# Gated linear recurrence in a hybrid layer: convolution by halves, the whole gate projection ahead of the block's products

## The chip, the cores and the metric

One core of a Trainium2 chip. The metric is the device time of one execution in microseconds (us), as the median of several runs.

## The reference, cut to what matters

One layer is computed for two sequences of 1024 tokens with the same weights. The normalised input is projected, four mixers work on columns of the projection, and their outputs are merged. Two mixers matter here. The gated linear recurrence (RG-LRU) has 512 channels in 4 blocks of 128:

```python
xc = centred_dwconv(u, conv_w) + conv_b            # 4 taps
xb = xc.reshape(bsz, L, LRU_BLOCKS, LRU_BLOCK_W)
for d, rev in enumerate((False, True)):
    r = sigmoid(einsum('blhi,hij->blhj', xb, w_a[d]) + b_a[d])
    i = sigmoid(einsum('blhi,hij->blhj', xb, w_x[d]) + b_x[d])
    log_a = -LRU_C * softplus(-lam[d]) * r
    drive = sqrt(-expm1(2.0 * log_a)) * (i * xc)
    _, h = associative_scan(_linear_combine, (exp(log_a), drive), axis=1, reverse=rev)
    hs.append(h)
return (hs[0] + hs[1]) * silu(gate)
```

The other is the gated delta rule. For each head and chunk of 64 tokens it needs the inverse of a unit triangular matrix (`triangular_solve(a_mat + eye, eye)`).

## The kernel before, in words

The whole kernel is one core's program. Channels lie on the 128 partitions and the 1024 tokens of a sequence along a row. An fp32 product is made of three: each operand is split into a high and a low part, and hi·hi, hi·lo and lo·hi are summed in a PSUM bank of 128x512. A projection of 128 channels is 2 halves of tokens with 24 matmuls each (`proj_steps`); each half ends in one bank with tag `pj`.

The change lies in a stage that each sequence goes through once. It has 3 `pj`, 2 `lr` and 3 `dn` banks. `weave` records three or four generators in turn, each by its declared length:

- `lru`: the four blocks of the recurrence, one after the other (`lru_block`, 8 calls in all);
- `cor`: the inverses of the delta rule for two pairs of heads (`dn_core1`, L540 to L676);
- early projections of gates for later stages (`pre_gates`; tiles `fg`, evicted by ACT and multiplied by DVE);
- in the first sequence, `s5_rot`, whose tiles are called `E`.

The order that is recorded is not yet the order on the engines. A scheduler reorders the instructions of the whole stage by its own estimate of their times, and then every engine (and SP, which issues most DMAs) works through its list strictly in order. So a matmul that is not ready holds up all matmuls behind it. Almost every instruction is recorded through one helper, so its line in the profile is L54; the names of tiles tell what it is.

A block of the recurrence projects its input into `up` (`conv_in`), convolves it on DVE into `xc` (one tensor_scalar and three scalar_tensor_tensor on 128x1024, `conv`), casts `xc` to its high part `xh` on ACT and subtracts on POOL for the low part `xl`. Then it records half of its gate projection (24 matmuls, evicted into `sg` by ACT and DVE), the first products of `r`, the other half of the gate, and the rest: for each direction `r` and `i`, two halves of 3 matmuls, each half in an `lr` bank that ACT empties with a sigmoid. ACT, POOL and DVE then form a, r and i, ending in a scan on DVE.

A pair in `dn_core1` is a chain. DVE forms the matrices from rows (`rl`, `sl`), PE multiplies the keys (`dn<-sl`), small diagonal blocks of 32x32 go to DRAM (`lan_d`, L582) and come back as `Nf` (L588). Then 31 steps of substitution run on DVE, two instructions each: `tm<-sl,sl` (a product) and `sl<-sl,tm` (a subtraction), with rows that grow from 31 to 256 elements and shrink again. The result goes to `lan_d` (L601) and comes back in pieces (L635), and only then can the matmuls `dn<-sl,LE` run, 8 for each direction of each head (the profile shows the 8 as x16). The text calls the first such group of a pair LE0 and the next one LE1.

Of the kernel before, what the change touches and what calls it, by code (L numbers as in the profile page):

```python
# [7 lines left out]
F32 = mybir.dt.float32  # L8
F32R = mybir.dt.float32r
I32 = mybir.dt.int32  # L10
AF = mybir.ActivationFunctionType
ALU = mybir.AluOpType
# [5 lines left out]
T = 1024  # L18
# [15 lines left out]
def tile_hybrid_trunk(ctx: ExitStack, tc: tile.TileContext, A):  # L34
# [55 lines left out]
    def after(i, j):  # L90

        tc.add_manual_dep(i.ins, j.ins.name,
                          mybir.DependencyInfo(mybir.DependencyClass.NoSync, mybir.DependencyReason.DATA),
                          reason="program order")

    def mm(*a, **kw):
        PE.matmul(*a, **kw)

    def transpose(*a):
        PE.transpose(*a)  # L100
# [1 line left out]
    def act(out, in_, func, **kw):  # L102
        return S.activation(out=out, in_=in_, func=func, **kw)

    def tt(eng, out, a, b, op):
        eng.tensor_tensor(out, a, b, op)

    def ts(eng, out, a, s1, s2, o1, o2=None):
        if o2 is None:
            eng.tensor_scalar(out, a, s1, None, o1)  # L110
        else:
            eng.tensor_scalar(out, a, s1, s2, o1, o2)

    def stt(out, a, s, b, o1, o2):
        V.scalar_tensor_tensor(out, a, s, b, o1, o2)
# [5 lines left out]
    HALVES = (slice(0, 512), slice(512, 1024))  # L121
# [107 lines left out]
    def run(gen):  # L229
        for _ in gen:  # L230
            pass
# [103 lines left out]
        proj_cm(xn, wp, w_in, c0, 128, evac)  # L335

    def conv(out, up, cw, bias=None, first=None):
        if first is S:
            act(out, up[:, 0:T], AF.Copy, scale=cw[:, 0:1])
        elif bias is None:  # L340
            ts(V, out, up[:, 0:T], cw[:, 0:1], None, ALU.mult)
        else:
            ts(V, out, up[:, 0:T], cw[:, 0:1], bias, ALU.mult, ALU.add)
        for j in range(1, 4):
            stt(out, up[:, j:j + T], cw[:, j:j + 1], out, ALU.mult, ALU.add)


    def misc(s, xn, wp, pl):
# [457 lines left out]
    def lru_block(s, b, xn, wp, pl):  # L806
        two = ("r", "i", "sg")
        wt = lambda shape, tag, dt=F32: pl.tile(shape, dt, tag=tag, name=nm(tag), bufs=2 if tag in two else 1)
        up = wt([128, T + 4], "up")
        conv_in(xn, wp, up, LRU_X + b * 128)  # L810
        yield
        xc = wt([128, T], "xc")
        conv(xc, up, lru_cw[:, b], lru_cb[:, b:b + 1])
        xh, xl = wt([128, T], "xh", F32R), wt([128, T], "xl", F32R)
        S.copy(xh, xc)
        tt(G, xl, xc, xh.bitcast(F32), ALU.subtract)

        def srcs(raw):
            v = raw[:, :512].rearrange("p (a d c) -> p a d c", a=2, d=2)
            yield v[:, 0], A["lru_w_a"][0, :, b].rearrange("d i j -> i d j")  # L820
            yield v[:, 1], A["lru_w_x"][0, :, b].rearrange("d i j -> i d j")
        hi, lo = split_tile(pl, 512, srcs, 512, "lw", 1, 1)
        sg = wt([128, T], "sg")
        gate = gate_steps(xn, wp, LRU_G + b * 128, sg)

        def half():
            for _ in range(8):
                next(gate, None)
        half()
        yield 0.4  # L830
        hv = []
        for d in range(2):
            gts = []
            for gi, bias in ((0, lru_ba), (1, lru_bx)):
                r = wt([128, T], ("r", "i")[gi])
                mi = slice((gi * 2 + d) * 128, (gi * 2 + d + 1) * 128)
                for hf in range(2):
                    sl = slice(hf * 512, (hf + 1) * 512)
                    p = bank("lr")
                    for n, (a, x) in enumerate(((hi, xh), (hi, xl), (lo, xh))):  # L840
                        mm(p, a[:, mi], x[:, sl], start=(n == 0), stop=(n == 2))
                    act(r[:, sl], p, AF.Sigmoid, bias=bias[:, d, b:b + 1])
                gts.append(r)
                if gi == 0:
                    if d == 0:
                        half()
                        run(gate)
                    yield 0.4
            r, ig = gts
            j = d * 4 + b  # L850
            tt(G, ig, ig, xc, ALU.mult)
            a = wt([128, T], "a")
            act(a, r, AF.Exp, scale=sp8n[:, j:j + 1])
            act(r, r, AF.Tanh, scale=sp8[:, j:j + 1])
            a2 = wt([128, T + 4], "up")[:, 0:T]
            act(a2, a, AF.Square)
            stt(r, a2, 1.0, r, ALU.add, ALU.mult)
            act(r, r, AF.Sqrt)
            tt(V, ig, ig, r, ALU.mult)
            if d == 0:  # L860
                V.tensor_tensor_scan(ig, a, ig, 0.0, ALU.mult, ALU.add)
            else:
                V.tensor_tensor_scan(ig[:, ::-1], a[:, ::-1], ig[:, ::-1], 0.0, ALU.mult, ALU.add)
            hv.append(ig)
            yield
        tt(G, hv[0], hv[0], hv[1], ALU.add)
        tt(V, sg, hv[0], sg, ALU.mult)
        put_y(sg, s, 0, b)
        yield 0.01
# [879 lines left out]
```

## Time and profile before

| | us |
|---|---|
| median of 3 runs (lowest to highest) | 3104.76 (3102.79 to 3108.0) |
| the profiled execution | 3103.76 |
| its span, first to last instruction | 3101.5 |
| PE busy in it | 2875.3 |
| mean granted TensorE clock | 0.966 |

The span stands 2.26 us below the time of the same execution. In the profile a line names the engine, the operation and the tiles it writes and reads (`out<-in`), and in brackets how long the engine stood idle before it and what released it. A clock of 1.00 is 2.4 GHz, 0.50 is 1.2 GHz. The stage of the first sequence lies at about 300 to 700 us of the span, that of the second at about 1780 to 2150 us.

### The profile page before, as it was taken

What the parts mean: (1) busy time and instruction counts of PE and PEld (TensorE: products, weight loads), DVE (VectorE), ACT (ScalarE), POOL (GpSimd) and SP (SyncE); (2) the same over time, 40 slices, a digit from 0 to 9 for tenths busy, and PEclk for the clock granted to TensorE, in tenths of its full rate; (3) what the DMA queues carried; (4) which work ended last, traced back from release to release, by engine and by line L of the source; (5) the groups of instructions that cost most, each with busy time, mean ns of one, the idle gap of its engine ahead of it and who ended that gap; (6) DMA issues with size and microseconds to landing.
All of it is one profiled execution on the core that took longest, in us unless ns stands there. A gap on an engine that the chain in (4) does not pass through costs nothing. (4 is left out here: it accounts for less than half of the span.)

```text
span 3101.5 us, 42101 instructions
## 1 busy us (share of the span) xinstructions
PE 2875.3 (93%) x15386; PEld 2373.6 (77%) x15386; DVE 1877.1 (61%) x3569; ACT 1286.2 (41%) x1969; POOL 1043.0 (34%) x796
## 2 busy tenths in 40 slices
PE   6999979898989999999999998989897999999998
PEld 5787767677778787878778876767776887788877
DVE  7576887738662464665654467773867245566545
ACT  5644546534432432332444465553443233333223
POOL 2343565434332231121443333343433212211123
PEclk9999989999999999999999998999998999999999
DMA  5344535353332754553553342524333263565343
GB/s 111 102 153 142 153 104 182 92 162 121 121 112 74 214 162 157 176 194 124 182 160 109 102 137 73 165 80 160 117 120 104 74 192 104 183 216 192 105 156 124
DMA packets 449391, 427.37 MB, mean 138 GB/s; under 512 B 126848, under 2 KB 340384, under 8 KB 449184
## 3 DMA queue, kind: packets, MB, share of 16 engines
q1 hardware_dynamic: 403200, 374.07, 39.2%
q10 hardware_dynamic: 45984, 50.61, 4.7%
q8 instruction: 121, 1.98, 0.3%
q14 instruction: 86, 0.70, 0.1%
HBM read 306.87 MB, written 117.70 MB: 137 GB/s over the span
## 5 line engine op out<-in xcount | busy, mean ns | idle before, releaser
L54 PE MATMUL pj<-xn,hi 128*128 128x512 f32 x4608 | 1471.2, 399 | 20.2 <-ACT y L54 5.7
L54 POOL TENSOR_TENSOR lo<-raw,hi 128x512 fp32r<-128x512 f32 x432 | 600.9, 1394 | 1451.8 <-ACT hi L54 1298.3
L54 PEld LDWEIGHTS pj<-xn,hi 128*128 128x128 f32 x4608 | 869.7, 191 | 206.1 <-ACT y L54 6.1
L54 PE MATMUL pj<-xn,lo 128*128 128x512 f32 x2304 | 912.5, 396 | 1.3 <-POOL lo L54 1.3
L54 ACT CAST hi<-raw 128x512 fp32r<-128x512 f32 x432 | 265.2, 618 | 650.8 <-PE pj L54 482.2
L54 PEld LDWEIGHTS pj<-xn,lo 128*128 128x128 f32 x2304 | 439.5, 191 | 99.5 <-issue 5.0
L54 ACT ACT_TABLE_LOAD x201 | 257.9, 1283 | 118.2 <-DVE Ab L54 54.6
L54 PE MATMUL pj<-yh,hi 128*128 128x512 f32 x576 | 239.8, 417 | 4.5 <-ACT yh L54 4.4
L54 PE MATMUL pj<-yl,hi 128*128 128x512 f32 x576 | 225.8, 393 | 1.0 <-DVE yl L54 1.0
L54 PE MATMUL pj<-yh,lo 128*128 128x512 f32 x576 | 226.0, 393 | 0.0
L54 DVE TENSOR_TENSOR_SCAN w<-E,v 64x512 f32<-64x512 f32 x64 | 97.9, 1529 | 85.2 <-PE s L54 84.3
L54 DVE TENSOR_TENSOR sg<-sg,pj 128x512 f32<-128x512 f32 x128 | 87.6, 684 | 93.4 <-PE pj L54 65.6
L54 PE MATMUL pj<-hi,mh 128*128 128x512 f32 x384 | 124.3, 400 | 6.7 <-ACT mh L54 4.1
L54 PEld LDWEIGHTS pj<-yh,hi 128*128 128x128 f32 x576 | 109.6, 190 | 23.9 <-ACT yh L54 5.2
L54 PEld LDWEIGHTS pj<-yh,lo 128*128 128x128 f32 x576 | 108.7, 189 | 23.8
L54 PEld LDWEIGHTS pj<-yl,hi 128*128 128x128 f32 x576 | 109.5, 190 | 19.9 <-DVE yl L54 2.6
L54 ACT ACTIVATE fg<-pj,bmg 128x512 f32<-128x512 f32 x112 | 76.3, 687 | 116.4 <-PE pj L54 104.2
L54 ACT ACTIVATE vn<-r,beta 128x128 f32<-128x128 f32 x128 | 40.7, 365 | 169.5 <-DVE vs L54 167.3
L54 POOL TENSOR_TENSOR dcv<-dcv,dsg 128x1024 f32<-128x1024 f32 x24 | 60.4, 2518 | 144.3 <-ACT dsg L54 103.5
L54 PE MATMUL pj<-hi,xn 128*128 128x256 f32 x512 | 97.9, 290 | 10.0 <-DVE vt L54 10.0
L54 DVE TENSOR_TENSOR yl<-yr,yh 128x512 fp32r<-128x512 f32 x80 | 59.9, 753 | 76.3 <-ACT yh L54 76.1
L54 DVE SCALAR_TENSOR_TENSOR dcv<-dup,dn_cw,dcv 128x1024 f32<-128x1024 f32 x72 | 96.0, 1333 | 5.5 <-ACT dcv L54 2.5
(373 smaller groups left out, 4469.1 us busy)
## 6 DMA issues: line engine op xcount, KB each, us to landing
raw<-in_w_in_dram SPq DMA_DIRECT2D x176, 256.0 KB, 2.9
sl<-rows_d SPq DMA_DIRECT2D x128, 256.0 KB, 6.5
raw<-in_w_merge_gate_dram SPq DMA_DIRECT2D x128, 256.0 KB, 2.9
gs_d<-fg ACTq DMA_DIRECT2D x112, 256.0 KB, 2.1
sg<-gs_d SPq DMA_DIRECT2D x112, 256.0 KB, 2.7
sl<-qkv_d SPq DMA_DIRECT2D x40, 512.0 KB, 5.5
raw<-in_w_branch_dram SPq DMA_DIRECT2D x64, 256.0 KB, 3.4
yr<-ysp SPq DMA_DIRECT2D x64, 256.0 KB, 3.1
```

Source lines behind the costliest of these rows:

```text
L54: i = f(*a, **kw)
```

## The change

The convolution works on halves of 512 tokens, and the cast and the subtraction follow each half. The whole gate projection is recorded ahead of the products. The first product of a block gets an order dependency (no semaphore) on the last matmul of the gate. What is computed stays the same.

```diff
@@ mm
+    lastmm = [None]
+
     def mm(*a, **kw):
-        PE.matmul(*a, **kw)
+        lastmm[0] = PE.matmul(*a, **kw)
+        return lastmm[0]
@@ conv
     def conv(out, up, cw, bias=None, first=None):
+        n = out.shape[1]
         if first is S:
-            act(out, up[:, 0:T], AF.Copy, scale=cw[:, 0:1])
+            act(out, up[:, 0:n], AF.Copy, scale=cw[:, 0:1])
...
         for j in range(1, 4):
-            stt(out, up[:, j:j + T], cw[:, j:j + 1], out, ALU.mult, ALU.add)
+            stt(out, up[:, j:j + n], cw[:, j:j + 1], out, ALU.mult, ALU.add)
@@ lru_block
-        conv(xc, up, lru_cw[:, b], lru_cb[:, b:b + 1])
         xh, xl = wt([128, T], "xh", F32R), wt([128, T], "xl", F32R)
-        S.copy(xh, xc)
-        tt(G, xl, xc, xh.bitcast(F32), ALU.subtract)
+        for sl in HALVES:
+            conv(xc[:, sl], up[:, sl.start:sl.stop + 3], lru_cw[:, b], lru_cb[:, b:b + 1])
+            S.copy(xh[:, sl], xc[:, sl])
+            tt(G, xl[:, sl], xc[:, sl], xh[:, sl].bitcast(F32), ALU.subtract)
...
         half()
+        half()
+        run(gate)
+        dense = lastmm[0]
         yield 0.4
...
-                        mm(p, a[:, mi], x[:, sl], start=(n == 0), stop=(n == 2))
+                        i = mm(p, a[:, mi], x[:, sl], start=(n == 0), stop=(n == 2))
+                        if dense:
+                            after(i, dense)
+                            dense = None
...
                 if gi == 0:
-                    if d == 0:
-                        half()
-                        run(gate)
                     yield 0.4
```

Since the scheduler orders the whole stage anew, more moves than the diff shows. Three places follow.

On PE, at the first products of block 1 of the first sequence (`pj_3700` and `pj_3756` are the two halves of that block's gate, `lr_` the banks of `r`), before:

```order
L54 MATMUL pj_3700<-xn_7_101,hi_3695 128x512 x2
L54 MATMUL pj_3700<-xn_7_101,lo_3696 128x512
L54 MATMUL lr_3744<-xh_3676,hi_3681 128x512
L54 MATMUL lr_3749<-xh_3676,hi_3681 128x512
L54 MATMUL pj_3756<-xn_0_94,hi_3689 128x512 x2
L54 MATMUL lr_3744<-xl_3677,hi_3681 128x512
L54 MATMUL lr_3744<-xh_3676,lo_3682 128x512
L54 MATMUL lr_3749<-xl_3677,hi_3681 128x512
L54 MATMUL lr_3749<-xh_3676,lo_3682 128x512
L54 MATMUL pj_3756<-xn_0_94,lo_3690 128x512
```

and in the changed kernel, where `pj_3739` is the second half of the gate:

```order
L54 MATMUL pj_3739<-xn_7_101,hi_3707 128x512 x2
L54 MATMUL pj_3739<-xn_7_101,lo_3708 128x512
L54 MATMUL lr_3785<-xh_3678,hi_3693 128x512
L54 MATMUL lr_3785<-xl_3679,hi_3693 128x512
L54 MATMUL lr_3785<-xh_3678,lo_3694 128x512
L54 MATMUL lr_3790<-xh_3678,hi_3693 128x512
L54 MATMUL lr_3790<-xl_3679,hi_3693 128x512
L54 MATMUL lr_3790<-xh_3678,lo_3694 128x512
L54 MATMUL pj_3856<-xn_0_94,hi_3845 128x512 x2
```

The products moved from behind the first half of the gate to behind both, 24 matmuls later.

On PE, around LE0 of the first pair of the first sequence (`dn_3900`), before:

```order
L54 MATMUL lr_4014<-xh_3676,lo_3682 128x512
L54 MATMUL pj_4059<-xn_0_94,hi_4048 128x512 x2
L54 MATMUL pj_4059<-xn_0_94,lo_4049 128x512
...
L54 MATMUL pj_4059<-xn_3_97,hi_4048 128x512 x2
L54 MATMUL pj_4059<-xn_3_97,lo_4049 128x512
L54 MATMUL dn_3900<-sl_3789,LE_3787 64x64 x8
L54 MATMUL pj_4059<-xn_4_98,hi_4054 128x512 x2
```

and in the changed kernel, where it is `dn_3912`:

```order
L54 MATMUL pj_3885<-xn_7_101,lo_3852 128x512
L54 MATMUL lr_4021<-xh_3678,hi_3693 128x512
L54 MATMUL lr_4021<-xl_3679,hi_3693 128x512
L54 MATMUL dn_3912<-sl_3801,LE_3799 64x64 x8
L54 MATMUL lr_4021<-xh_3678,lo_3694 128x512
L54 MATMUL lr_4026<-xh_3678,hi_3693 128x512
```

LE0 moved 16 matmuls forward in PE's list: 12 of a projection and 4 products now stand behind it. In the first pair of the second sequence it moved 8 forward, and in the second pairs it kept its place (LE0 of the first sequence is PE's row 1543 in both lists).

On DVE, at the end of the substitution of the same pair (`tm` and `sl`; `r_3743` is the `r` of block 1, `sg` and `fg` products of gates), before:

```order
L54 TENSOR_TENSOR tm_3731<-sl_3314,sl_3315 128x135
L54 SCALAR_TENSOR_TENSOR r_3743<-up_3822,r_3743 128x1024
L54 TENSOR_TENSOR sl_3315<-sl_3315,tm_3731 128x27x5
L54 TENSOR_TENSOR sg_3687<-sg_3687,pj_3756 128x512
...
L54 TENSOR_TENSOR tm_3783<-sl_3314,sl_3315 128x31
L54 TENSOR_TENSOR sl_3315<-sl_3315,tm_3783 128x31
L54 TENSOR_TENSOR i_3807<-i_3807,r_3743 128x1024
```

and in the changed kernel:

```order
L54 TENSOR_TENSOR sl_3321<-sl_3321,tm_3772 128x27x5
L54 TENSOR_TENSOR sg_3699<-sg_3699,pj_3739 128x512
...
L54 TENSOR_TENSOR tm_3795<-sl_3320,sl_3321 128x31
L54 TENSOR_TENSOR sl_3321<-sl_3321,tm_3795 128x31
L54 SCALAR_TENSOR_TENSOR r_3784<-up_3834,r_3784 128x1024
L54 TENSOR_TENSOR fg_3881<-fg_3881,pj_3856 128x512
```

The work on `r` moved behind the last step of the substitution. At the other end of this chain another `r` (of block 0) moved out too, ahead of the first step.

## Rows read from the trace of the kernel before

**Rows 1.** The page, part 1: busy time of each engine.

```profile
PE 2875.3 (93%) x15386; PEld 2373.6 (77%) x15386; DVE 1877.1 (61%) x3569; ACT 1286.2 (41%) x1969; POOL 1043.0 (34%) x796
```

**Rows 2.** PE's waits at 300 to 700 us: total us, times, longest.

```profile
PE lr L54 <- ACT xh L54: 16.2, 3, 7.5
PE lr L54 <- ACT r L54: 5.4, 1, 5.4
...
PE lr L54 <- POOL xl L54: 2.3, 2, 1.8
```

**Rows 3.** PE's waits at 1780 to 2160 us, same columns.

```profile
PE lr L54 <- ACT xh L54: 7.3, 1, 7.3
...
PE lr L54 <- POOL xl L54: 4.0, 2, 2.2
```

**Rows 4.** ACT's timeline: start us, us, engine, line, operation, idle before.

```profile
400.16 1.04 ACT L54 CAST xh<-xc 128x1024 fp32r<-128x1024 f32 x1 [15.59 <-DVE xc L54]
```

**Rows 5.** Windows; columns in the first line.

```profile
core 0: us, PE busy (x) PEld busy (x) DVE busy (x) ACT busy (x) POOL busy (x), PEclk, DMA share, GB/s
390.00:420.00 30.00, 20.79 (x73) 16.05 (x74) 29.42 (x37) 13.35 (x16) 22.41 (x28) 0.77 0.30 96
401.20:409.80 8.60, 8.03 (x18) 5.87 (x19) 8.32 (x11) 5.32 (x8) 8.21 (x13) 0.50 0.22 63
435.50:440.50 5.00, 4.97 (x25) 4.11 (x26) 4.76 (x17) 4.93 (x7) 0.61 (x1) 0.50 0.43 113
578.10:584.00 5.90, 4.11 (x9) 2.92 (x10) 5.76 (x5) 3.66 (x7) 5.34 (x3) 0.50 0.22 74
602.60:610.00 7.40, 5.37 (x50) 4.42 (x50) 5.79 (x6) 4.14 (x8) 5.88 (x5) 1.00 0.64 186
1888.10:1894.70 6.60, 4.81 (x11) 3.44 (x12) 6.43 (x6) 5.41 (x8) 5.37 (x3) 0.50 0.34 81
```

**Rows 6.** PE's timeline, LE0 and LE1 of three pairs and a cadence.

```profile
435.53 1.12 PE L54 MATMUL dn<-sl,LE 128*64 128x64 f32 x16 [4.44 <-DMA sl<-lan_d]
...
600.50 0.61 PE L54 MATMUL pj<-xn,hi 128*128 128x512 f32 x2
600.96 0.40 PE L54 MATMUL pj<-xn,lo 128*128 128x512 f32 x1
...
602.67 0.69 PE L54 MATMUL dn<-sl,LE 128*64 128x64 f32 x16
605.38 0.69 PE L54 MATMUL dn<-sl,LE 128*64 128x64 f32 x16 [2.03 <-POOL lo L54]
...
1912.43 1.12 PE L54 MATMUL dn<-sl,LE 128*64 128x64 f32 x16 [5.30 <-DMA sl<-lan_d]
...
2080.40 0.69 PE L54 MATMUL dn<-sl,LE 128*64 128x64 f32 x16 [2.96 <-DMA sl<-lan_d]
```

**Rows 7.** DVE's timeline, first pair, first sequence.

```profile
364.19 0.19 DVE L54 TENSOR_TENSOR tm<-sl,sl 128x31 f32<-128x31 f32 x1
...
423.05 1.21 DVE L54 SCALAR_TENSOR_TENSOR r<-up,r 128x1024 f32<-128x1024 f32 x1
...
427.02 0.21 DVE L54 TENSOR_TENSOR sl<-sl,tm 128x31 f32<-128x31 f32 x1
```

**Rows 8.** DVE's timeline, second pair, first sequence.

```profile
570.32 0.60 DVE L54 TENSOR_TENSOR tm<-sl,sl 128x255 f32<-128x255 f32 x1
...
578.46 2.54 DVE L54 TENSOR_TENSOR tm<-sl,sl 128x247 f32<-128x247 f32 x1
...
593.02 0.67 DVE L54 TENSOR_TENSOR sg<-sg,pj 128x512 f32<-128x512 f32 x1
...
595.24 0.22 DVE L54 TENSOR_TENSOR sl<-sl,tm 128x31 f32<-128x31 f32 x1
```

**Rows 9.** DVE's timeline, start of the first pair's chain, second sequence.

```profile
1855.46 0.21 DVE L54 TENSOR_TENSOR tm<-sl,sl 128x31 f32<-128x31 f32 x1 [4.25 <-DMA sl<-lan_d]
...
1856.37 1.22 DVE L54 SCALAR_TENSOR_TENSOR r<-up,r 128x1024 f32<-128x1024 f32 x1
```

More of the change, by code (lines that the diff above doesn't have):

```diff
@@ L337, in conv @@
     def conv(out, up, cw, bias=None, first=None):
+        n = out.shape[1]
         if first is S:
-            act(out, up[:, 0:T], AF.Copy, scale=cw[:, 0:1])
+            act(out, up[:, 0:n], AF.Copy, scale=cw[:, 0:1])
         elif bias is None:
-            ts(V, out, up[:, 0:T], cw[:, 0:1], None, ALU.mult)
+            ts(V, out, up[:, 0:n], cw[:, 0:1], None, ALU.mult)
         else:
-            ts(V, out, up[:, 0:T], cw[:, 0:1], bias, ALU.mult, ALU.add)
+            ts(V, out, up[:, 0:n], cw[:, 0:1], bias, ALU.mult, ALU.add)
         for j in range(1, 4):
-            stt(out, up[:, j:j + T], cw[:, j:j + 1], out, ALU.mult, ALU.add)
+            stt(out, up[:, j:j + n], cw[:, j:j + 1], out, ALU.mult, ALU.add)
     def misc(s, xn, wp, pl):
```

## The prediction

> **What bounds the kernel now.** I read the page's busy times first. PE is busy for 93% of the span and DVE for 61% [rows 1], so over the whole kernel the question is what makes PE idle. The waits of PE in the two stages that the change touches give the answer at first sight: products of the recurrence (`lr`) wait for the cast `xh`, for an `lr` bank that ACT has to empty (`r`) and for the low part `xl`. That is 16.2 + 5.4 + 2.3 = 23.9 us in the first sequence [rows 2] and 7.3 + 4.0 = 11.3 us in the second [rows 3], 35.2 us together (three smaller groups left aside).
>
> Then I asked why `xh` is late. ACT had stood idle for 15.59 us before the cast of block 1, waiting for DVE [rows 4]. DVE, in turn, is busy for 29.42 of the 30 us around it, and PE in the same window for only 20.79 [rows 5]: the convolution stands in DVE's list among the steps of a pair's substitution. So the stage has a second chain beside PE. The substitution of the first pair runs on DVE from 364.19 to 427.02 us [rows 7], its result goes out to DRAM and back, and PE meets it at LE0, where it waits again: 4.44 us in the first pair, nothing at LE0 and 2.03 us at LE1 in the second, 5.30 us in the first pair of the second sequence and 2.96 us at LE1 of the last [rows 6]. In these rows PE, with all its stalls, is still ahead of the chain at three pairs and level with it at the fourth. What the stalls cost is therefore not their sum: a PE without them comes to LE earlier and waits there.
>
> Last, the clock. After the three long waits for `xh` the granted clock is 0.50 for 8.6, 5.9 and 6.6 us, and after the 4.44 us at LE0 it is 0.50 for 5.0 us; after the second pair's LE0, which PE reached without a wait, it is 1.00 [rows 5]. 0.50 is the level of 1.2 GHz.
>
> **The change part by part.** *The tie and the early gate* add no instruction to any queue and no semaphore; both halves' weights are loaded, cast and split by one group of DMAs, ACT casts and POOL subtractions before the change too, so no DMA is added on SP and none is moved past another by this edit itself. What moves is 24 matmuls of a gate, with one sigmoid on ACT and one product on DVE, ahead of the products. At one matmul per (600.96 - 600.50) / 2 = 0.23 us [rows 6] that is 24 x 0.23 = 5.5 us of work for PE while it would have waited for `xh`. *The halves* let the first cast start after four operations of 512 instead of 1024, and add 4 instructions on DVE, one on ACT and one on POOL per block. A 512-wide DVE operation takes 0.67 us [rows 8] and a 1024-wide scalar_tensor_tensor 1.21 [rows 7], so each of the four splits adds 2 x 0.67 - 1.21 = 0.13 us: 0.5 us per block, all of it inside the chain that counts. Together these two edits should remove nearly all waits for `xh`, and the products of block 0 run some 3 us sooner. By the argument above, all that appears at LE.
>
> So the sum is made at the four LEs: when does the chain deliver, and what does PE still have to do behind it?
>
> First pair, first sequence. Block 0 delivers its scans about 2 us earlier (it waited 5.4 us for an `r` bank [rows 2]; the halves take part of that, between 0 and 5.4, and I take 2). One `r` of 1.21 us leaves the chain at its end [rows 7], by the list of the changed kernel, and a second one of the same kind leaves it at the start, where it now stands before the first step and uses up part of the earlier scan. With the halves' 0.5 us the chain ends 2 + 1.21 + 1.21 - 0.5 = 3.9 us earlier, at least 0 and at most 7.3 (with all 5.4). But LE0 stands 16 matmuls further forward in PE's list, and what PE no longer does ahead of it, 16 x 0.23 = 3.7 us, it has to do behind it. Net -0.2 us. PE's wait there becomes long: it came at 435.53 - 4.44 = 431.1; without 7.5 us for `xh`, the half of 8.03 us at 0.50, those 3.7 us and the 2 of block 0 it comes at about 414, and LE0 runs at about 431.6.
>
> Second pair, first sequence. The chain's order is the same up to 0.5 us for the halves and one more gate product of 0.67 us [rows 8] ahead of its end: +1.2 us. PE reached LE0 at 602.67 with no wait; without 7.5 + 1.8 us of waits [rows 2] and half of 4.11 us at 0.50 [rows 5] it comes about 11 us early, so it idles instead and then runs at the low level. The nearest row is the 5.0 us after LE0 of the first pair: half of it lost would be 2.5 us. About 2.0 us of it fall into the wait at LE1 that is there already [rows 6], so I take 1.5, between 0 and the 4.3 that half of 8.6 us gives. Net +2.7 us.
>
> First pair, second sequence. There DVE waits 4.25 us for the DMAs that bring the small blocks back before the chain can start [rows 9]. In the new lists an `r` of 1.22 us moves from inside the chain into this wait [rows 9], and the last matrices, which follow block 0's scan now, should be done some 1.8 us sooner, since the products ahead of that scan wait less. With the halves' 0.5 us the end comes 1.22 + 1.8 - 0.5 = 2.5 us earlier, between 0 and the whole 4.25. 8 matmuls, 1.8 us, stand behind LE0 that stood ahead of it. Net -0.7 us; the low clock after its wait is there before and after.
>
> Second pair, second sequence. Its longest removable wait is the 2.2 us for `xl` [rows 3]. PE waits for LE1 already; +0.5 us for the halves and 0.5 for the clock (0 to 2.5): +1.0 us.
>
> The sum is -0.2 + 2.7 - 0.7 + 1.0 = +2.8 us on the profiled execution's 3103.76: 3106.6 us. This execution lies 1.0 us below the median of the runs shown, which is inside their spread, so I leave it there.
>
> **Rivals.**
>
> *A, the stalls come back in full.* If LE were not the meeting point, PE would gain the 35.2 us and half of its 8.03 + 4.11 + 4.81 us at the low level [rows 5], 8.5 us: 3103.8 - 43.7 = 3060 us. For it speaks DVE's 61%; against it the 29.42 of 30 us and the waits at LE. The Trainium skill, Perfetto Trace Analysis, section Optimizing Scalar/DVE Operations, says that instructions of ScalarE and VectorE that are not saturated but cause bubbles elsewhere may be broken up so that work completes sooner, and that larger operations help where the engine is saturated. By its first half this rival would hold, at 3060 us; by its second the halves are a loss, and the window at 390 to 420 us bears out the second.
>
> *B, the chain itself gets shorter.* DVE's steps are stretched while POOL works: the product of 247 elements at 578.46 took 2.54 us, just behind `xh`'s cast, against 0.60 for one of 255 elements at 570.32 [rows 8]. If the two halves of `xl` fall beside work that is not stretched, the step and the two behind it, some 3 us per block, go away at three or four chains, 9 to 12 us, and the low clock costs nothing: about 3094 us. Against it: POOL's own work stays, and lies beside the same chain.
>
> *C, slower: LE doesn't come earlier, yet its work was moved.* In the first pairs 24 matmuls stand behind LE that stood ahead of it. If the chains end when they did before, 3.9 + 2.5 = 6.4 us of my sum are gone, and 3106.6 + 6.4 = 3113 us; with the clock's upper price (4.3 instead of 1.5 and 2.5 instead of 0.5) 3118. It decides at 3.7 and 1.8 us: if the chain's ends gain less than that in the two first pairs, the move loses. For it speaks that DVE has almost no idle time in which to gain, and that gate products (`sg`) stay in the chain; against it the two `r` that left.
>
> That the change doesn't do what it says I give no chance: the lists show the products behind both halves of the gate.
>
> **How the numbers follow.** A measurement of this kernel can tell about 0.2%, 6.2 us, from no change. The forecast gets 0.50, of which 0.37 within that bound (3098.6 to 3111.0 about the median), 0.11 slower and 0.02 faster, since its terms can miss by some 4 us each. A gets 0.07, B 0.22 (0.17 faster, 0.05 same), C 0.21 (0.17 slower, 0.04 same). So faster 0.26, same 0.46, slower 0.28. The range leaves out A and the outer ends of B and C: 3086 to 3119.
>
> **What would show it.** In the profile of the changed kernel the waits of `lr` for `xh` should be gone but for a few us in the two stages, and waits of `dn` for `sl<-lan_d` (or for `pj` banks just ahead) should have grown to 10 to 20 us in each first pair and about 10 us in the second pair of the first sequence. The substitution's last step should end near 423 in the first pair and a little behind 595 in the second, LE0 should run near 431 and 603 to 604. I am wrong if LE0 of the first pairs comes 10 us earlier (B), or if the products' waits vanish with no new wait at LE (A); C shows as LE0 near 435 and the same work behind it.

## The result and the profile after

The changed kernel took 3122.8 us (median of 4 runs, 3119.7 to 3128.3) beside 3106.4 us of the kernel before in the same rounds: ratio 1.0054 [1.0041, 1.0067]. Ten later runs of it gave 3117.9 us (3112.5 to 3122.4), ratio 1.0042 [1.0029, 1.0056]. So it is slower by 13 to 16 us, 0.4 to 0.5%. The median of the first four runs lies outside the range that I gave (3086 to 3119 around 3106.6); that of the ten later runs lies 1 us inside its upper end.

The page of the kernel after, part 1. PE does the same work as before [rows 1]; DVE, ACT and POOL were busy for 6 to 10 us more, with the split instructions among it:

```profile
PE 2874.8 (92%) x15386; PEld 2371.4 (76%) x15386; DVE 1883.9 (60%) x3601; ACT 1291.8 (41%) x1980; POOL 1053.2 (34%) x804
```

PE's waits of the kernel after at 300 to 700 us, beside [rows 2] (total us, times, longest):

```profile
PE dn L54 <- DMA sl<-lan_d: 14.1, 4, 10.7
PE pj L54 <- DVE fg L54: 6.5, 1, 6.5
PE lr L54 <- ACT i L54: 5.5, 3, 3.4
PE pj L54 <- DVE sg L54: 5.5, 1, 5.5
PE lr L54 <- ACT r L54: 5.2, 3, 2.8
...
PE lr L54 <- ACT xh L54: 3.2, 1, 3.2
```

And at 1780 to 2160 us, beside [rows 3]:

```profile
PE dn L54 <- DMA sl<-lan_d: 12.8, 1, 12.8
PE lr L54 <- ACT i L54: 7.8, 1, 7.8
PE lr L54 <- ACT r L54: 5.3, 4, 2.8
```

The change did what it says. The waits for `xh` fell from 16.2 to 3.2 us in the first sequence, and from 7.3 to none in the second; those for `xl` are gone. In their place PE waits for the substitution's result (`sl<-lan_d`), for banks that ACT has to empty (`i`, `r`), and for `pj` banks whose gate product (`sg`, `fg`) stands in DVE's list.

The stage's end, read at the first `gl` matmul behind it, stands at 709.47 us instead of 694.57. A window from 300 us to that end holds the same 1935 matmuls in both kernels. Before:

```profile
core 0: us, PE busy (x) PEld busy (x) DVE busy (x) ACT busy (x) POOL busy (x), PEclk, DMA share, GB/s
300.00:694.57 394.57, 349.40 (x1935) 280.04 (x1933) 276.17 (x517) 195.43 (x275) 198.11 (x196) 0.94 0.46 141
```

and after:

```profile
300.00:709.47 409.47, 356.73 (x1935) 285.45 (x1933) 279.06 (x533) 200.98 (x282) 199.93 (x200) 0.93 0.44 136
```

The profiled span grew by 3118.0 - 3101.5 = 16.5 us, and 14.9 us of it are there at the end of this stage, so nearly all of the loss is made in the first sequence's stage. It has two halves. PE stood idle for 52.7 us instead of 45.2, 7.6 more, and it was busy for 356.7 us instead of 349.4 with the same matmuls, 7.3 more, at a mean granted clock of 0.93 instead of 0.94.

The four meeting points, PE's timeline of the kernel after, beside [rows 6]:

```profile
434.20 1.12 PE L54 MATMUL dn<-sl,LE 128*64 128x64 f32 x16 [10.74 <-DMA sl<-lan_d]
...
616.71 0.78 PE L54 MATMUL dn<-sl,LE 128*64 128x64 f32 x16 [1.17 <-DMA sl<-lan_d]
...
1923.03 1.12 PE L54 MATMUL dn<-sl,LE 128*64 128x64 f32 x16 [12.85 <-DMA sl<-lan_d]
...
2092.10 1.98 PE L54 MATMUL dn<-sl,LE 128*64 128x64 f32 x32
```

LE0 of the first pair came 1.3 us sooner than before, behind a wait of 10.74 us instead of 4.44. LE0 of the second pair came 14.0 us later (616.71 instead of 602.67). The loss is made between these two. PE has 2844 matmuls ahead of the second LE0 in both kernels; up to there it was busy for 4.1 us more and idle for 10.0 us more. At LE0 itself it waits for only 1.17 us. It had been held up 12 us earlier:

```profile
604.36 1.22 PE L54 MATMUL pj<-xn,hi 128*128 128x512 f32 x2 [5.52 <-DVE sg L54]
```

The bank that it waits for there is freed by a gate product (`sg`, at 603.62 on DVE), and this product stands in DVE's list among the steps of the second pair's substitution. So a late substitution reaches PE by way of the gates too, not at LE alone.

### The profile page after: what moved, and what is told of

Same layout as the page of the kernel before. It is cut to its first block, busy times and chain, and to the rows that moved or that the text cites. A ratio compares the mean times of both kernels' runs of the same rounds, so it can differ in the third digit from the quotient of the medians.

```text
span 3118.0 us, 42175 instructions
## 1 busy us (share of the span) xinstructions
PE 2874.8 (92%) x15386; PEld 2371.4 (76%) x15386; DVE 1883.9 (60%) x3601; ACT 1291.8 (41%) x1980; POOL 1053.2 (34%) x804
## 5 line engine op out<-in xcount | busy, mean ns | idle before, releaser
L54 PE MATMUL pj<-hi,xn 128*128 128x256 f32 x512 | 98.8, 292 | 10.7 <-DVE vt L54 10.7
```

The source lines that it names most:

```text
L54: i = f(*a, **kw)
```

## Where the second pair loses its time

The second pair's substitution took as long as before, some 44 us, but its first step starts at 566.26 us instead of 551.05. Four engines' lists lead there. DVE of the kernel after:

```profile
522.54 1.13 DVE L54 SCALAR_TENSOR_TENSOR sl<-sl,scl,m_sl 128x128 f32<-128x128 f32 x4
...
541.89 1.23 DVE L54 TENSOR_TENSOR i<-i,r 128x1024 f32<-128x1024 f32 x1 [6.55 <-POOL i L54]
...
560.93 1.23 DVE L54 TENSOR_TENSOR i<-i,r 128x1024 f32<-128x1024 f32 x1 [9.27 <-POOL i L54]
...
566.26 2.33 DVE L54 TENSOR_TENSOR tm<-sl,sl 128x31 f32<-128x31 f32 x1 [1.78 <-POOL sl L54]
```

DVE waits for POOL three times, 17.6 us together. Before, it waited twice for the products, 12.2 us together, and not at the first step (DVE of the kernel before):

```profile
530.71 1.62 DVE L54 TENSOR_TENSOR i<-i,r 128x1024 f32<-128x1024 f32 x1 [6.45 <-POOL i L54]
...
547.53 1.22 DVE L54 TENSOR_TENSOR i<-i,r 128x1024 f32<-128x1024 f32 x1 [5.76 <-POOL i L54]
...
551.05 1.17 DVE L54 TENSOR_TENSOR tm<-sl,sl 128x31 f32<-128x31 f32 x1
```

POOL of the kernel after:

```profile
539.48 2.38 POOL L54 TENSOR_TENSOR i<-i,xc 128x1024 f32<-128x1024 f32 x1 [10.55 <-ACT i L54]
...
558.50 2.40 POOL L54 TENSOR_TENSOR i<-i,xc 128x1024 f32<-128x1024 f32 x1
...
566.07 0.15 POOL L54 MEMSET sl<- 128x32 f32 x1
566.15 2.39 POOL L54 TENSOR_TENSOR i<-i,i 128x1024 f32<-128x1024 f32 x1
```

The last releaser of the substitution is a memset: it writes the ones on the diagonal of the slab into which the inverse is built. It needs nothing of the gate, but it stands in POOL's list behind the product of `i` and `xc`, and POOL had stood idle for 10.55 us waiting for `i`. Before, this wait took 2.42 us (POOL of the kernel before):

```profile
528.29 2.38 POOL L54 TENSOR_TENSOR i<-i,xc 128x1024 f32<-128x1024 f32 x1 [2.42 <-ACT i L54]
```

So ACT comes next. ACT of the kernel after:

```profile
523.71 1.06 ACT L54 ACTIVATE sl<-sl 128x1024 f32<-128x1024 f32 x1 [3.53 <-DVE sl L54]
...
527.17 0.68 ACT L54 ACTIVATE r<-lr,lru_ba 128x512 f32<-128x512 f32 x1
...
534.34 0.69 ACT L54 ACTIVATE i<-lr,lru_bx 128x512 f32<-128x512 f32 x1
...
538.72 0.69 ACT L54 ACTIVATE i<-lr,lru_bx 128x512 f32<-128x512 f32 x1
```

and ACT of the kernel before:

```profile
513.65 1.27 ACT L54 ACTIVATE r<-lr,lru_ba 128x512 f32<-128x512 f32 x2
...
519.80 1.05 ACT L54 ACTIVATE sl<-sl 128x1024 f32<-128x1024 f32 x1
...
526.95 1.27 ACT L54 ACTIVATE i<-lr,lru_bx 128x512 f32<-128x512 f32 x2
```

Before, the eviction of block 2's `r` stands ahead of the second pair's last exponential (`sl<-sl`); now it stands behind it. That exponential waits 3.53 us for rows of the decay that DVE still has to write (the last at 522.54), and `r`, then both halves of `i`, then POOL's product, the memset and the first step wait with it. The swap can't be the whole delay: on PE the products of that `r` began at 518.36 us instead of 505.66, so 12.7 us later already. The experiments ask what the swap costs, and what makes it happen.

## The experiments

Times are medians; the kernel before gave 3103.6 to 3104.8 us in them. Numbers of "the first step" are those of the second pair in the first sequence, 551.05 before and 566.26 after. In the texts that were put down before each run, T names the theory that I held then (at first that the gate ahead of block 2's products makes the second pair's chain start late, later that the start of each pair's chain sets the time), H that the halves' extra instructions cost the time, and W that the low clock does.

**Each part alone.** First the halves without the early gate (the gate's second half goes back between the products):

```diff
-        half()
-        run(gate)
-        dense = lastmm[0]
...
+                    if d == 0:
+                        half()
+                        run(gate)
```

> The convolution, cast and subtraction by halves alone; the gate is projected half ahead and half behind the first r products, as before. Theory T (the gate ahead of block 2's products delays the block's scan, and the second pair's chain stands behind that scan on DVE): block 2's products stand where they stood before (both have 1620 matmuls of 512 columns ahead of them), so LE0 of the second pair in the first sequence runs within 3 us of 602.7 and the time is that of the kernel before, 3101 to 3109 us. Theory H (the halves' extra instructions lengthen the chain on DVE): slower than before by 8 us or more, 3114 to 3122.

Measured: 3115.1 us, 1.0035 [1.0024, 1.0046]. The halves alone cost 10 us, where I had taken 0.5 us per block. The time is that of theory H, but the second pair's substitution did not get longer by much (45.2 us against 44.4); it starts at 571.69. DVE of this kernel at the first pair shows one place:

```profile
376.44 1.22 DVE L54 SCALAR_TENSOR_TENSOR r<-up,r 128x1024 f32<-128x1024 f32 x1 [6.55 <-ACT up L54]
377.58 1.28 DVE L54 TENSOR_TENSOR tm<-sl,sl 128x31 f32<-128x31 f32 x1
```

Block 0's second `r` multiply stands ahead of the first pair's first step and waits for ACT; the step starts at 377.58 instead of 364.19 [rows 7].

Then the early gate and its tie, with the convolution whole:

```diff
-        for sl in HALVES:
-            conv(xc[:, sl], up[:, sl.start:sl.stop + 3], lru_cw[:, b], lru_cb[:, b:b + 1])
-            S.copy(xh[:, sl], xc[:, sl])
-            tt(G, xl[:, sl], xc[:, sl], xh[:, sl].bitcast(F32), ALU.subtract)
+        conv(xc, up, lru_cw[:, b], lru_cb[:, b:b + 1])
+        S.copy(xh, xc)
+        tt(G, xl, xc, xh.bitcast(F32), ALU.subtract)
```

> The gate ahead alone; the convolution is whole, as before. Theory T: block 2's products have 1644 matmuls ahead of them as in the change, 24 more than before, and the second pair's LE0 in the first sequence comes 8 to 15 us late: 3115 to 3123 us. Theory H: without the halves the loss is gone, 3103 to 3109 us.

Measured: 3118.6 us, 1.0046 [1.0027, 1.0064], first step at 564.2. The early gate alone has the late second pair, and again `r`'s eviction (529.03) stands behind the last exponential (525.56). The two parts cost 10 and 14 us apart and 13 to 16 together: they don't add up, since each moves the order that the other works on.

**Which block.** The change, but block 2's gate half ahead and half between as before:

```diff
+        whole = b != 2
+        dense = None
+        if whole:
+            half()
+            run(gate)
+            dense = lastmm[0]
...
+                    if d == 0 and not whole:
+                        half()
+                        run(gate)
```

> The change, but in block 2 of each sequence half of the gate goes behind the first r products again. Theory T: the second pair's chain starts 6 to 12 us earlier than in the change in the first sequence and some 3 us earlier in the second: 3107 to 3115 us. Theory H and theory W (PE loses time at the low clock after its long waits at LE): nothing of that depends on block 2, 3119 to 3126 us.

Measured: 3107.9 us, 1.0011 [0.9998, 1.0024], first step at 559.3, `r`'s eviction at 516.7, ahead of the last exponential (522.99). Some 10 us of the loss need block 2's early gate.

The halves everywhere, the early gate in blocks 1 and 3 alone (`whole = b in (1, 3)` in the same edit):

> The halves everywhere, the gate ahead only in blocks 1 and 3, whose first products waited for the cast before. Theory T: as with block 2 alone undone, and block 0 starts as before too, so that the first pair's chain starts as early as before or earlier: 3105 to 3113 us. Theories H and W: 3117 us or more.

Measured: 3129.2 us, 1.0079 [1.0057, 1.0100], a miss for theory T and slower than the change: without block 0's early gate its halves put the first pair's first step at 378.8, as in the run with halves alone. Both edits in blocks 1 and 3 alone:

```diff
-        for sl in HALVES:
+        for sl in (HALVES if b in (1, 3) else (slice(0, T),)):
...
+        whole = b in (1, 3)
```

> Halves and early gate in blocks 1 and 3 alone, the two whose first products waited for the cast; blocks 0 and 2 as before. On DVE the order around the start of both chains of the first sequence is then letter for letter that of the kernel before. Theory T (the time is set by when each pair's chain starts on DVE, behind operations of blocks 0 and 2): the waits for the cast go, the waits at LE grow by as much, LE0 runs within 3 us of 435.5 and 602.7, and the time is that of the kernel before, 3101 to 3110 us. Rival A of the prediction (the stalls come back): 25 us or more faster, below 3080. Theory H (the halves cost on DVE): 3111 or more.

Measured: 3110.5 us, 1.0018 [1.0004, 1.0031], first step at 558.1. So the two edits gain nothing even in the blocks where `xh` was waited for. LE0 came at 439.4 and 608.4, 4 and 6 us later than before, where theory T allowed 3. Here `r`'s eviction came at 513.15, no later than before, and the chain started 7 us late all the same: the exponential behind it (519.33) waited 3.62 us for DVE, and `i` came at 531.00 instead of 526.95. In the first stage PE's wait for `xh` (1.8 us left) is replaced, in about the same size, by the wait for the next thing. PE's waits at 300 to 700 us; before, the same three were 2.3, 5.4 and nothing:

```profile
PE lr L54 <- ACT i L54: 11.6, 3, 10.2
PE lr L54 <- ACT r L54: 6.6, 3, 4.5
PE pj L54 <- DVE sg L54: 5.0, 1, 5.0
```

And block 2's early gate alone, on the kernel before (`whole = b == 2`, convolution whole). My first theory, T, was that 24 matmuls more ahead of block 2's products are enough to make its gate late:

> The kernel before with one thing changed: in block 2 of each sequence the whole gate is projected ahead of the products. The convolution is whole everywhere and blocks 0, 1 and 3 are as before. In PE's list block 2's products stand 24 matmuls later, and all LE groups keep their places; on DVE the second pair's last matrices now stand behind two of block 2's operations instead of one. Theory T: 24 matmuls at 0.23 us are 5.5 us by which the products and the second chain start later, and the matrices' new place adds some: the chain starts at 556 to 566 instead of 551 in the first sequence, its LE0 comes 5 to 14 us late, and the time is 3110 to 3122 us. If the loss of the change came from the halves or from block 0: 3101 to 3108.

Measured: 3103.3 us, 1.0001 [0.9989, 1.0013], first step at 550.0. Theory T fell. Its products did come 8 us later (513.8 instead of 505.7), but ACT shows where that went:

```profile
518.46 0.68 ACT L54 ACTIVATE r<-lr,lru_ba 128x512 f32<-128x512 f32 x1
...
521.03 1.06 ACT L54 ACTIVATE sl<-sl 128x1024 f32<-128x1024 f32 x1
...
526.58 1.27 ACT L54 ACTIVATE i<-lr,lru_bx 128x512 f32<-128x512 f32 x2
```

`r`'s eviction came 4.8 us later and still ahead of the last exponential, and `i` at 526.58 instead of 526.95: there was slack. Theory T2 came of this: it takes two delays. One is that DVE's decay rows for the second pair end later, by 6.4 us with the change in all blocks but 2 and by 7.5 us with both edits in blocks 1 and 3 alone (times 3 and 6 us above before). The other is block 2's early gate, which delays `r`. By T2 only both together put `r`'s eviction behind an exponential that waits. The runs agree with that, but none has the early gates of blocks 1 and 3 without the halves, and with block 2's early gate alone the rows end 4.4 us later too.

**Shorter chains by other means.** If the chain on DVE set the time, giving the pair's work more of the turns should help the change (the weight of the pair's core in the weave 30 to 44):

```diff
-                todo = [(30, cor), (16, lru), *early(s, NP[s][2], 0.15, xn, wp, fp)]
+                todo = [(44, cor), (16, lru), *early(s, NP[s][2], 0.15, xn, wp, fp)]
```

> The change whole, with the declared length of the pairs' generator raised from 30 to 44, so that the second pair is recorded ahead of block 2's recurrence: on DVE all its matrices and its first step stand ahead of block 2's first r, where the change has them behind two of block 2's three operations. Theory T: the second chain starts at least 15 us earlier than in the change (566.3), LE0 of that pair runs before 602, and the time falls to 3095 to 3112 us although block 2's gate still stands ahead. If the loss were in the early gate, the halves or the clock themselves, it stays at 3117 or more.

Measured: 3115.0 us, 1.0036 [1.0025, 1.0047]. The first step came at 534.2 and the last began at 592.8, before the 595.24 of [rows 8]. PE waited 15.85 us at LE0 all the same, which came at 599.3, and the stage ended at 709.56, as in the change. The same edit on the kernel before:

> The kernel before with the same length of 44 for the pairs. Theory T: the second chain's start (551.1) comes earlier here too, by 5 to 15 us, but PE reached that LE without waiting, so little of it is gained: 3090 to 3106 us. If the chain is nothing that counts: 3104 to 3112.

Measured: 3103.8 us, 0.9999 [0.9989, 1.0009], with LE0 at 592.6 and the stage's end at 700.8, 6 us later than before. And on the kernel with both edits in blocks 1 and 3:

> Halves and early gate in blocks 1 and 3 alone, with the length of 44. Theory T: now the chain of the second pair is early and PE's stall ahead of its LE is gone too, so the two gains should add where neither did alone: 3080 to 3100 us, at least 5 us below the kernel before with the length of 44. Rival: no better than that kernel.

Measured: 3118.5 us, 1.0046 [1.0028, 1.0064]: a miss. An early start by a larger share of the turns buys nothing in these three runs: what the chain gains is gone again by the end of the stage.

A bound on the chain itself: the kernel before with steps 10 to 19 of each substitution left out:

```diff
             nj, nt_ = x + 1, 31 - x
+            if 10 <= x < 20:
+                continue
```

> The kernel before with 10 of the 31 steps of every substitution left out (steps 10 to 19, the widest), so that its inverses are not those of the reference: 20 DVE operations and some 10.5 us less in each of the four chains. Theory T: the chains set the time before the change too, so the time falls by 15 to 40 us, more than the 14.7 us that PE was seen to wait at the four LE: 3065 to 3090 us. If PE alone sets the time: 3095 or more.

Measured: 3104.1 us, 1.0001 [0.9992, 1.0010], 14 us above the upper end of what I expected. Its LE0s came at 420.7 and 580.9, 15 and 22 us sooner, and the stage ended 7 us later. PE's waits of this kernel at 300 to 700 us:

```profile
PE dn L54 <- DMA sl<-lan_d: 14.9, 3, 9.3
PE pj L54 <- ACT fg L54: 9.9, 2, 8.8
```

The order was made anew for the shorter chain: LE moved forward in PE's list (1930 and 2710 matmuls run ahead of the two LE0, instead of 1992 and 2844) and met the chain again. So shortening the substitution by itself bought nothing here, as removing PE's waits by themselves bought nothing; each experiment has to be read with the order that it got.

**The gate's chain.** POOL's product of `i` and `xc` is a link of the path found above. The kernel before, with that product on DVE in blocks 0 and 2:

```diff
-            tt(G, ig, ig, xc, ALU.mult)
+            tt(V if b in (0, 2) else G, ig, ig, xc, ALU.mult)
```

> The kernel before with the product i*xc of blocks 0 and 2 on DVE instead of POOL, where DVE waited 6.45 and 5.76 us for it ahead of the second chain. PE's list is the same around both chains. Theory T: the second chain starts 4 to 10 us earlier than 551, but PE reached its LE0 without waiting, so only the waits at LE1 and behind can shrink: 3097 to 3105 us. If the chain's start is nothing that counts: 3103 to 3108, and if DVE's added work counts more: 3108 or more.

Measured: **3086.7 us** (3081.7 to 3095.1, 6 runs), 0.9947 [0.9932, 0.9962]: it beats both kernels by 17 and 31 us. The first step came 5.9 us earlier, as theory T had it, but the time lies 10 us below the range that I expected. DVE of this kernel:

```profile
522.90 1.27 DVE L54 TENSOR_TENSOR i<-i,xc 128x1024 f32<-128x1024 f32 x1 [2.94 <-ACT i L54]
...
545.20 0.71 DVE L54 TENSOR_TENSOR tm<-sl,sl 128x31 f32<-128x31 f32 x1 [3.13 <-DMA sl<-lan_d]
```

The product took 1.27 us on DVE instead of 2.4 on POOL. The first step came at 545.20, and what it waited for is the transfer of the blocks that it works on; the waits of 6.45 and 5.76 us for POOL's products ahead of it are gone. LE0 came at 430.7 and 595.4. The first stage ended at 687.84, 6.7 us sooner than before, and another 6 us were gained by the end of the second sequence's stage, so about half of the gain lies behind the chain that I followed.

The same move with both edits in blocks 1 and 3:

> Halves and early gate in blocks 1 and 3 alone, with the product i*xc of blocks 0 and 2 on DVE. Theory T: the chains start earlier and PE's stalls ahead of LE are gone, so part of the stalls comes back: 3090 to 3102 us, 5 us or more below both the same kernel without the move (3110.5) and the move alone. Rival: the time follows the sum of the two single effects, about 3105 to 3111.

Measured: 3103.2 us, 1.0003 [0.9994, 1.0013], a miss: I expected it 5 us below the move alone, and on this base the two edits in blocks 1 and 3 cost 16 us. It also lies 2 us below the rival's sum.

**The disputed order by itself.** On the changed kernel, one dependency more: the second pair's last exponential has to stand behind the first eviction of block 2's `r`.

```diff
-                act(Ld, Ld, AF.Exp, scale=-1.0 if d == 0 else 1.0)
+                ex = act(Ld, Ld, AF.Exp, scale=-1.0 if d == 0 else 1.0)
+                if pair == 1 and hh == 1 and d == 1:
+                    after(ex, pin[s])
...
-                    act(r[:, sl], p, AF.Sigmoid, bias=bias[:, d, b:b + 1])
+                    ev = act(r[:, sl], p, AF.Sigmoid, bias=bias[:, d, b:b + 1])
+                    if b == 2 and d == 0 and gi == 0:
+                        pin[s] = ev
```

> The whole change, and one order more: the last exponential of the second pair (ACT, sl<-sl 128x1024) has to stand behind the first eviction of block 2's r products, as it does before the change; nothing else moves on PE or DVE ahead of it. Theory T2 (the 24 matmuls and the recurrence of block 1 that ends later put r's eviction behind an exponential that waits for DVE, and i, the next gate, the second pair's matrices follow): r's eviction at 520 to 523 instead of 527, the second pair's first step at 556 to 561 instead of 566.3, time 3106 to 3114. Rival (the place of the eviction is a bystander, DVE has more work ahead of the pair): first step at 564 to 568, time 3119 to 3126.

Measured: 3111.5 us (12 runs), 1.0024 [1.0011, 1.0036]. ACT of this kernel:

```profile
520.32 0.68 ACT L54 ACTIVATE r<-lr,lru_ba 128x512 f32<-128x512 f32 x1
...
525.10 1.06 ACT L54 ACTIVATE sl<-sl 128x1024 f32<-128x1024 f32 x1 [2.22 <-DVE sl L54]
...
530.65 1.27 ACT L54 ACTIVATE i<-lr,lru_bx 128x512 f32<-128x512 f32 x2
```

and its POOL and DVE:

```profile
532.00 2.40 POOL L54 TENSOR_TENSOR i<-i,xc 128x1024 f32<-128x1024 f32 x1 [0.91 <-ACT i L54]
```

```profile
559.46 2.33 DVE L54 TENSOR_TENSOR tm<-sl,sl 128x31 f32<-128x31 f32 x1 [1.22 <-POOL sl L54]
```

All of T2's numbers came as expected: `r` at 520.3, the first step at 559.5, the time. The exponential still waits for DVE (2.22 us, and runs 1.4 us later than in the change), but block 2's `r` no longer waits with it; POOL's idle time falls from 10.55 to 0.91 us. This one added dependency is worth 6.4 us against the change's ten later runs (made in other rounds), about half of the loss. The rival (the eviction's place is a bystander) is out. More than the two instructions moved with it on ACT: two table loads of 1.28 us each fell away in this stretch, and the two halves of `i` are evicted together (530.65, x2) instead of apart (534.34 and 538.72). So the 6.4 us are the price of the order that the dependency gives, not of the eviction alone.

The other order: block 0's second `r` multiply behind the first pair's first step.

```diff
+            rr = stt(r, a2, 1.0, r, ALU.add, ALU.mult)
+            if b == 0 and (s, 0) in pin2:
+                after(rr, pin2[s, 0])
...
+            sub = tt(V, xv, xv, tv, ALU.subtract)
+            if x == 0:
+                pin2[s, pair] = sub
```

> The whole change, and one order more: block 0's second r multiply on DVE (r<-up,r) stands behind the first pair's first substitution step, as it does before the change, instead of ahead of it, where it waited 4.7 us for ACT. If that wait is a price of the change, the first pair's first step is at 364 to 366 instead of 369.2, its last about 4 us earlier, and the time 3116 to 3120. Rival (matmuls that move up fill the front, and the later waits take it back, as when the substitution was cut): first step earlier as said, but the time 3121 to 3126.

Measured: 3115.9 us, 1.0037 [1.0024, 1.0050]. DVE of this kernel:

```profile
368.19 0.21 DVE L54 TENSOR_TENSOR tm<-sl,sl 128x31 f32<-128x31 f32 x1 [5.02 <-POOL sl L54]
```

The first step gained 1.0 us, not 4: POOL's memset of the diagonal ends at 368.1 to 368.2 in this kernel as in the change (start 368.00 and 367.96, 0.16 us long), so the step could not have started sooner. The wait for ACT only hid a wait for POOL. And the last step, which I expected 4 us earlier, came 2 us later (429.05). Both orders together, and the change once more in the same rounds:

> The change with both orders put back: the second pair's last exponential behind r's eviction, and block 0's second r multiply behind the first pair's first step. The first pair's first step only came 1.0 us earlier with the second order (POOL was waited for 5.0 us instead), so the first order alone counts: 3108 to 3113, second pair's first step at 557 to 561. If the two add up: 3104 to 3107.

> The change itself once more, in the same rounds as the next kernel. Its first four runs gave 3119.7 to 3128.3; the experiments stand some us lower than those in their own rounds, so that the price of the change may be nearer 12 to 15 us than 16.4: 3116 to 3122. If it comes out at 3116 or less, putting back block 0's r multiply (3115.9) was worth nothing.

Measured: 3107.6 us, 1.0016 [1.0004, 1.0028], first step at 557.9; the change itself 3117.9 us, 1.0042 [1.0029, 1.0056], first step at 565.9. The second order's part, 2 to 4 us, is no larger than the intervals, so I leave it open.

Last, the move of `i` and `xc` on top of the change, and with the pinned exponential:

> The whole change, with the product of i and xc of blocks 0 and 2 on DVE instead of POOL (the move that took 17 us off the kernel before). If the two do not touch each other: 3103 to 3109. If they do, as they did with blocks 1 and 3 alone (there the move gave 7 us): 3112 to 3119. Theory T2 has it that block 2's gate chain is what is late, so that the move gives at least as much as without the change: 3100 to 3109.

> The two edits together: the change, the second pair's last exponential behind r's eviction, and the product of i and xc of blocks 0 and 2 on DVE. By theory T2, 8 us for the order and 7 to 17 for the move: 3094 to 3107, so not below 3086.7, the kernel before with the move alone. Rival (the change is harmless once these two are mended): 3082 to 3090.

Measured: 3107.3 us, 1.0012 [1.0000, 1.0024], and 3107.5 us, 1.0010 [0.9997, 1.0023]. The move gives 10.6 us with the change; the pin then gives nothing more, so the two do not add as T2 had it (3094 to 3107). That fits one path with two ways to shorten it: with POOL out of the way the first step is released by a transfer (557.7 and 558.3), whatever ACT's order is. That the change still stands 21 us above the kernel before with the same move I can't account for link by link, but the profiles show where PE fell behind. With the change it reached the second LE0 at 613.4 us without a wait, 18 us later than in the kernel before with the move (595.4, without a wait too), although the substitution's last step was at 599.7. So it was not this chain that held PE there. Its waits at 300 to 615 us were 17.1 us for `lr` banks that ACT has to empty of `i` (2.3 without the change), 6.9 for `fg` and 4.8 for `sg` (none without it), against 2.8 for `xh` instead of 10.7.

## Why the prediction was wrong

- **Right: the waits for `xh` go, and PE meets LE instead.** 16.2 us became 3.2, and the first pairs' waits at LE0 became 10.74 and 12.85 us (10 to 20 forecast). The second sequence's terms, +0.3 us in all, are not far off: its first matmuls are 12.6 us late (1586.02 instead of 1573.46) and the end of its stage 14.6, so +2.0. Rival A, with the stalls coming back in full, is out.
- **Wrong: "Second pair, first sequence. The chain's order is the same up to 0.5 us for the halves and one more gate product."** I priced that chain from DVE's list of its steps alone and took its start for granted. The steps did keep their length, but the start moved by 15.2 us, through ACT (`r` behind the last exponential), POOL (`i` and `xc`, then the memset) and DVE. My term was +2.7 us; LE0 moved by +14.0. The pinned run shows 6.8 us of the start's delay to come of ACT's order. The rest, 8.4 us, is there in the runs that leave block 2's gate or the order as it was (first step at 558 to 559.5, times 3 to 7.5 us above before); what makes it is argued from the waits, not shown by a run that takes it away alone. And the chain is not all: on its way to LE0 PE also waited for banks, 6.5 us for `fg` (none before) and 5.5 for `i` (2.3 before), for which my sum has no term.
- **Wrong, but small in time: "a second one of the same kind leaves it at the start, where it now stands before the first step and uses up part of the earlier scan."** That `r` waited 4.69 us for ACT and the first step started 5.0 us later, so the chain ended at 427.09 instead of 423 as forecast, no sooner than before. DVE of the kernel after:

```profile
367.82 1.28 DVE L54 SCALAR_TENSOR_TENSOR r<-up,r 128x1024 f32<-128x1024 f32 x1 [4.69 <-ACT up L54]
...
369.22 0.21 DVE L54 TENSOR_TENSOR tm<-sl,sl 128x31 f32<-128x31 f32 x1
```

Counting an instruction of 1.2 us as moved, without asking what it waits for at its new place, was the error; the later run adds that POOL's memset would have held the step until 368.2 anyway.
- **Rival C was the nearest.** Its condition held in the first pair of the first sequence: the chain's end gained nothing, and 16 matmuls stand behind LE. In the second sequence it did not hold: there the chain ended 10.1 us later where the sequence began 12.6 us late, so 2.5 us sooner, as forecast. Its prices, 3113 to 3118, hold the median of the later ten runs by luck: the main loss is in the second pair, where it put none but the clock. Rival B (a shorter chain, 3094) found no support: the first pair's steps took 5 us less, but they began 5 us later, and the second pair's took as long as before.
- **The clock.** In the 5 us behind LE0 the granted clock was 0.50 again, and in the 7.4 us behind the second pair's LE0 0.54 instead of 1.00 [rows 5], as I had feared. Windows of the kernel after:

```profile
434.20:439.20 5.00, 5.00 (x25) 4.08 (x26) 4.93 (x3) 1.99 (x5) 4.87 (x7) 0.50 0.23 69
616.70:624.10 7.40, 5.76 (x41) 4.70 (x42) 6.50 (x6) 3.54 (x8) 6.88 (x5) 0.54 0.47 135
```

Half of 5.76 us at the low level would be 2.9 us, twice the 1.5 that I took, and within its bounds. But I priced the clock behind LE alone. Over the whole first stage the same matmuls kept PE busy for 7.3 us more, and for that my sum has no term.

What stays open: why a first step that comes 17 us sooner by a larger share of the turns (534.2) gives nothing, while one that comes 6 us sooner by a lighter POOL goes with a gain of 17 us, only some 7 of them in this stage. The start of one substitution is thus a sign of the loss here and not its measure. Whether a memset placed earlier in POOL's list would help the changed kernel by itself was not tried.

## What to carry to other kernels

Before you price a chain by the length of its steps, ask what releases its first step, and follow that back through every engine's list to an instruction that waits for another unit; each list is run in order, so a cheap instruction behind a waiting one costs that wait. A stall that you remove on the busiest engine is worth only as much as the next thing that this engine waits for comes earlier. To find out which swap counts, undo the change block by block and pin single orders. An engine that is busy for a third of the time can still hold the path: here moving one product off POOL took 17 us off the kernel before, while the change itself cost 13 to 16.

## What I had not expected of the chip

A DVE operation stretched to the end of a POOL operation. The first step of the second pair, a product of 128x31, took 2.33 us at 566.26, where POOL ran `i<-i,i` from 566.15 for 2.39 us: 568.59 and 568.54 as ends. In the pinned kernel it took 2.33 us as well, beside a POOL product from 559.35 for 2.40 (561.79 and 561.75). Without such a neighbour it took 0.19 us [rows 7]. POOL of the pinned kernel:

```profile
559.35 2.40 POOL L54 TENSOR_TENSOR i<-i,i 128x1024 f32<-128x1024 f32 x1
```

The Trainium skill, SBUF — State Buffer, section SBUF: two separate sides, says that a DVE operation with two SBUF inputs and a GpSimd operation that reads SBUF share a pair of ports, and that the first to start holds it for its whole instruction. The two ends above agree with it to 0.05 us. The Trainium skill, Perfetto Trace Analysis, section Optimizing Scalar/DVE Operations, draws from the shared port that moving operations between these two engines might not help; the run with `i` and `xc` on DVE speaks against that for this kernel, at 1.27 instead of 2.4 us for the product and 17 us less for the whole.
